# A FoX and RWKV-7 layer on one core: two operands turned by TensorE instead of VectorE and DMA

## The chip, the cores and the metric

The kernel runs on one core of one Trainium2 chip, in one launch. The metric is the time on the device in microseconds (us). The engines have short names in the profile: PE is TensorE (matmuls and transposes, PEld its weight loads), DVE is VectorE, ACT is ScalarE, POOL is GpSimd, and SP is SyncE, which issues nearly all transfers (DMAs).

## The reference

One layer on 256 frames of width 4096: a projection, two kinds of token mixing, a gate, an output projection and a normalised residual.

```python
proj = jnp.einsum('bsd,dc->bsc', x, w_in)
...
logits = jnp.einsum('bhqd,bhkd->bhqk', qb, kf) + cb[..., :, None] - c[..., None, :]
logits = jnp.where(key_pos[None, :] <= q_pos[:, None], logits, -jnp.inf)
p = jax.nn.softmax(logits, axis=-1)
return jnp.einsum('bhqk,bhkd->bhqd', p, vf)
...
sa = jnp.einsum('bhvk,bhk->bhv', state, a_t)
state = (state * w_t[:, :, None, :] + sa[..., None] * b_t[:, :, None, :]
         + v_t[..., None] * k_t[:, :, None, :])
return state, jnp.einsum('bhvk,bhk->bhv', state, r_t)
...
h = jnp.concatenate([fox_out, rwkv_out], axis=-1) * jax.nn.silu(z.astype(f32))
out = jnp.einsum('bsc,cd->bsd', h.astype(x.dtype), w_out)
x = _layernorm(ALPHA * x.astype(f32) + out.astype(f32), ln_gain, ln_bias, LN_EPS).astype(x.dtype)
```

The first three quoted parts are the projection, the forgetting attention ("fox", 16 heads of 128) and the RWKV-7 recurrence (32 heads of 64). All of it is float32.

## The kernel before, in words

**The projection sets the frame.** `w_in` is worked off in eight iterations n = 0 to 7 of four blocks b = 0 to 3, each 512 columns wide. A block is 16 chunks of weights, 512 KB each. A chunk arrives by a DMA on SP (`load`, four buffers), ACT casts it to a high half (`split`, L140, four buffers), and DVE subtracts that from the original for the low half (L141). TensorE then runs 12 matmuls of 128x512 per chunk (`mm`, L146 to L148: high by high, low by high, high by low). In the trace the halves are called `w_7h` and `w_7l` for chunk 7, whatever the block.

**The mixing runs beside it.** Every other pair of three matmuls `block` calls `slot()`, which advances each generator in `sides` by one step; a generator that yields n times (`wait(n)`, with the table `W`) so puts its next instructions n slots later in the program. Each iteration brings two RWKV groups (block 0 gives r and k, block 1 v) and two attention heads: head 2n from block 2, head 2n+1 from block 3. The generators are `prepare` (operands of the recurrence), `rwkv` (the recurrence), `unload` (turning a block's result), and `fox` (one attention head). A scheduler then orders the instructions of every engine by when it expects them to be ready; each engine works its queue in order, and a waiting instruction holds all behind it.

**In `rwkv`** the factors BK (128 x 2 x 4 chunks x 128) feed the products `gp` (L517), are scaled by POOL (L519, three of the four chunks), and are wanted transposed as `BKt` in the chunk-by-chunk recurrence (`up`, L653). They are turned in two stages: DVE transposes their 32x32 squares in place (L547), and DMAs carry the squares to their places, four to a DRAM buffer (`turn`) and one back. These DMAs are issued in `turns()`, a generator that advances with each step of the solve loop. That loop (L577 to L585) inverts the unit triangles: 31 steps of a product `prod` (L579) and a sum `xc` (L582) on DVE. It falls into block 3. The triangle's other helpers, `vt` and `bon` (L565), follow in `turns()`.

**In `fox`** the probabilities `lg` (three blocks of 128x128: DVE L722, L723, L726, ACT's exponential L724) are wanted transposed as `pT` for the product with the values, `fop` (L744, L745). For heads 0 to 13 this is done with DVE squares (L728), `turn` and a DMA back; for heads 14 and 15 with three TensorE transposes into PSUM (`fpt`, L739) and one ACT copy (L740). ACT copies `fop` out as `fo` (L747), and the gate follows.

After the iterations the output projection runs (`wo`, 128 chunks), with the residual and the norm.

Of the kernel before, what the change touches and what calls it, by code (L numbers as in the profile page):

```python
# [10 lines left out]
F32 = mybir.dt.float32  # L11
# [6 lines left out]
P = 128  # L18
# [66 lines left out]
def layer(ctx: ExitStack, tc: tile.TileContext, xt, xtok, w_lora, w_main, muv, w_o, up, par, mulora, fbias, lng, lnb, cst, out):  # L85
    nc = tc.nc
# [8 lines left out]
    def pst(name):  # L95
        return ps.tile([P, 512], F32, tag="ps", name=name)
# [34 lines left out]
    ident = cs[:, C_ID : C_ID + P]  # L131
    ones = cs[:, C_ONES : C_ONES + P]

    def column(name, i):
        return prm[:, PAR.index(name), i : i + 1]
# [21 lines left out]
    for n, (k0, k1) in enumerate(pieces):  # L157
        for k in range(k0, k1):
            t = xpool.tile([P, 2, S], F32R, tag=f"x{k}", name=f"x{k}")
# [31 lines left out]
    def wait(n):  # L191
        for _ in range(n):
            yield
# [67 lines left out]
    rp = mid.enter_context(tc.tile_pool(name="rp", bufs=1))  # L261
# [18 lines left out]
    def issue(out, src):  # L280
        tc.keep_in_program_order(nc.sync.dma_start(out=out, in_=src))

    def turn(src, name, each=2):
        _, m, cols = src.shape
        d = dram.tile([cols // B, B, m, 4, B], F32, tag=f"dt{m}_{cols}", name=name, bufs=2)
        s = src.rearrange("p m (q t) -> p m q t", t=B)
        for a in range(4):
            issue(d[:, :, :, a, :].rearrange("q i m t -> i m q t"), s[B * a : B * (a + 1)])
            if a % each == each - 1:
                yield  # L290
        return d
# [103 lines left out]
    def flat(t):  # L395
        return t.rearrange("p a b -> p (a b)")
# [108 lines left out]
    def rwkv(n):  # L505
# [3 lines left out]
        q = pairs[n]  # L509
        lc, BK, lt, bon = q["lc"], q["BK"], q["lt"], q["bon"]  # L510
# [9 lines left out]
        p, t = bks[n], vs_[n]  # L520
# [22 lines left out]
        SV = [rp.tile([P, 2, NCH, C], F32, tag=f"SV{j}", name=f"SV{j}_{n}") for j in range(2)]  # L543
        UV = [rp.tile([P, 2, NCH, C], F32, tag=f"UV{j}", name=f"UV{j}_{n}") for j in range(2)]
        yield from wait(W["tp"])
        for u in range(2):
            tc.keep_in_program_order(nc.vector.transpose(flat(BK[:, u]), flat(BK[:, u])))  # L547
        yield from wait(W["d1"])
        BKt = rp.tile([P, 2, NCH, P], F32, tag="shl", name=f"BKt{n}")

        def turns():
            d = yield from turn(BK.rearrange("p u c t -> p (u c) t"), f"BKt{n}", 1)
            yield from wait(2)
            issue(BKt.rearrange("p u c t -> p (u c t)"), d.rearrange("q i g a t -> (q i) (g a t)"))
            yield
            vst = UV[0].rearrange("p u c v -> p (u c v)").rearrange("p (m q) -> p m q", m=2)
            for a in range(2):
                tc.keep_in_program_order(nc.vector.transpose(vst[:, a, :], vs_[n][:, a, :]))
            yield from wait(3)
            d = yield from turn(vst, f"vt{n}", 1)  # L560
            yield from wait(2)
            vv[n] = rp.tile([P, 2, S], F32, tag="s2", name=f"vv{n}")
            issue(vv[n], turned_back(d))
            yield from wait(4)
            nc.vector.tensor_tensor(flat(bon), flat(bon), flat(vv[n]), ALU.mult)  # L565
            for u in range(2):
                nc.scalar.activation(bon[:, u], bon[:, u], AF.Identity, bias=column("gn_bias", i0 + u))
            bonned.add(n)
# [43 lines left out]
        for u in range(2):  # L612
            for c in range(NCH):
                for j in range(2):
                    a, b = slice(C * j, C * j + B), slice(C * j + B, C * j + C)
# [91 lines left out]
    def fox(i, q, k, vt):  # L707
        nb = rp.tile([P, 3, P], F32, tag="nb", name=f"nb{i}")
        row = ncd[i : i + 1, :]
        nc.sync.dma_start(out=flat(nb[:, 0:1, :]), in_=row[:, :P].to_broadcast([P, P]))  # L710
        nc.sync.dma_start(out=flat(nb[:, 1:3, :]), in_=row.to_broadcast([P, S]))
        for m in (0, 2):
            nc.gpsimd.affine_select(out=nb[:, m, :], in_=nb[:, m, :], compare_op=ALU.is_ge, fill=NEG, base=0, pattern=[[-1, P]], channel_multiplier=1)
        yield from wait(W["fs"])
        sp = pst(f"fsp{i}")
        nc.tensor.matmul(sp[:, :P], q[:, :P], k[:, :P], start=True, stop=True)
        nc.tensor.matmul(sp[:, P : 3 * P], q[:, P:], k, start=True, stop=True)
        lg = rp.tile([P, 3, P], F32, tag="lg", name=f"lg{i}")
        spv = sp[:, : 3 * P].rearrange("p (a t) -> p a t", t=P)
        st = rp.tile([P, 6], F32, tag="fst", name=f"fst{i}", bufs=2)  # L720
        for m, blk in enumerate((slice(0, 1), slice(1, 3))):
            nc.vector.scalar_tensor_tensor(lg[:, blk, :], spv[:, blk, :], ct[:, m * NF + i : m * NF + i + 1], nb[:, blk, :], ALU.add, ALU.add)  # L722
            nc.vector.tensor_reduce(st[:, m : m + 1], lg[:, blk, :], AX.XY, ALU.max, negate=True)  # L723
            nc.scalar.activation(lg[:, blk, :], lg[:, blk, :], AF.Exp, bias=st[:, m : m + 1], accum_out=st[:, 2 + m : 3 + m])  # L724
            nc.vector.reciprocal(st[:, 4 + m : 5 + m], st[:, 2 + m : 3 + m])
            nc.vector.tensor_scalar(lg[:, blk, :], lg[:, blk, :], st[:, 4 + m : 5 + m], None, ALU.mult)  # L726
        if i < G - 2:
            nc.vector.transpose(flat(lg), flat(lg))  # L728
        yield from wait(W["fp"])
        if i < G - 2:  # L730
            ld = yield from turn(lg, f"fpt{i}")
            yield
        pT = rp.tile([P, 3 * P], F32, tag="nb", name=f"pT{i}")
        if i < G - 2:
            issue(pT, ld.rearrange("q i m a t -> (q i) (m a t)"))
        else:
            pt = pst(f"fpt{i}")
            for m in range(3):
                nc.tensor.transpose(pt[:, m * P : (m + 1) * P], lg[:, m, :], ident)  # L739
            nc.scalar.copy(pT, pt[:, : 3 * P])  # L740
        yield from wait(W["fo"])
        op = pst(f"fop{i}")
        f = slice(i % 2 * P, i % 2 * P + P)
        nc.tensor.matmul(op[:, :S], vt[:, 0, f], pT[:, :S], start=True, stop=False)  # L744
        nc.tensor.matmul(op[:, P:S], vt[:, 1, f], pT[:, S:], start=False, stop=True)  # L745
        o = t256("fq", f"fo{i}")
        nc.scalar.copy(o, op[:, :S])  # L747
        while f"f{i}" not in szs or 2 * i >= FAR and not closed:
            yield
        yield from gate(o, f"f{i}", 2 * i)  # L750
        foxed.add(i)
# [17 lines left out]
    def turned_back(d):  # L769
        return d.rearrange("(u b) i m a t -> u (b i) (m a t)", b=4).rearrange("u p s -> p u s")  # L770
# [148 lines left out]
    for b, q in outs:  # L919
        if q == 0:  # L920
            pool, tag = (ps, "ps") if b == 1 or b and b % 2 == 0 else (pp, "pp")
# [91 lines left out]
    z0, _, last = moments(0)  # L1013
# [79 lines left out]
```

## Time and profile before

| | us |
|---|---|
| three runs, median (lowest to highest) | 1992.68 (1992.07 to 1992.7) |
| the profiled execution, its span | 1990.4 |
| what the median has over that span | 2.3 |
| one iteration, between first `gp` matmuls (n = 2 to n = 3) | 198.0 |
| PE busy | 1948.0 |
| DVE busy | 1384.1 |
| ACT busy | 962.3 |

The profiled execution has no time of its own beside its span; the runs' median is 2.3 us above it. Busy times are shares of the span: a TensorE matmul counts as busy while it runs, at full clock or not. The views that carry the argument stand in the prediction: the page, the list of waits, the timeline, the windows, and groups of instructions of one line (with count, shortest, median and longest duration in ns).

### The profile page before, as it was taken

To read this page: it belongs to the slowest core of one execution; us is meant where nothing else is said; L and a number is where in the kernel's file an instruction comes from. 1 tells how busy PE (TensorE), PEld (TensorE's weight loads), DVE (VectorE), ACT (ScalarE), POOL (GpSimd) and SP (SyncE) were. 2 spreads that over 40 slices of the span, in tenths; PEclk is the share of its full clock that TensorE was granted. 3 is DMA by queue.
4 is the path that set the end of the run, shared out by engine and by line. 5 is a ranking of instruction groups with operands and counts; after the bars stand their busy time and mean duration, and the time that the engine had idled before them with its cause. 6 is when DMAs were issued, how large, how long until landed. Compare 5 with 4: busy or idle time off the path is not lost.

```text
span 1990.4 us, 28153 instructions
## 1 busy us (share of the span) xinstructions
PE 1948.0 (98%) x10063; PEld 1583.7 (80%) x10063; DVE 1384.1 (70%) x2242; ACT 962.3 (48%) x1455; POOL 79.6 (4%) x111
## 2 busy tenths in 40 slices
PE   9998999999999999999999999999999999999998
PEld 8887787788777887778777877787778878888886
DVE  6577658865886588668866886688668856755555
ACT  6552555355535554455355544554455445443333
POOL 0010001000100010001000100010001000000000
PEclk9999999999999999999999999999999999999999
DMA  9577676867786769677867786778676877866664
GB/s 335 150 230 218 196 196 214 237 205 201 224 240 202 211 212 247 201 204 213 251 200 200 219 248 198 201 221 246 197 203 210 262 281 234 259 200 200 196 190 169
DMA packets 328241, 434.03 MB, mean 218 GB/s; under 512 B 198370, under 2 KB 228852, under 8 KB 328100
## 3 DMA queue, kind: packets, MB, share of 16 engines
q1 hardware_dynamic: 327668, 431.81, 72.3%
q8 instruction: 79, 1.29, 0.3%
q14 instruction: 62, 0.51, 0.1%
q10 hardware_dynamic: 432, 0.43, 0.1%
HBM read 395.56 MB, written 36.59 MB: 217 GB/s over the span
## 4 chain that ended last, share of the span: by engine, by line
PE 85%; DVE 11%; issue 2%; ACT 1%; DMA 1%; ACTq 0%; DVEq 0%; SPq 0%
PE acc L146 20%; PE acc L148 20%; PE acc L147 19%; PE oacc L860 6%; PE oacc L861 6%; PE oacc L862 6%; DVE prod L579 3%; DVE xc L582 3%; PE yp L678 1%; PE gp L517 1%; DMA w<-in_w_main_dram 1%; PE up L653 1%; PE rh L626 1%; DVE w_7l L141 1%; DVE w_15l L141 0%
## 5 line engine op out<-in xcount | busy, mean ns | idle before, releaser
L582 DVE TENSOR_REDUCE xc<-prod 128x8 f32<-128x16 f32 (+30 forms) x248 | 72.8, 294 | 7.0
L579 DVE TENSOR_TENSOR prod<-Nb,xc 128x8 f32<-128x8 f32 (+30 forms) x248 | 72.1, 291 | 7.0
L141 DVE TENSOR_TENSOR w_0l<-w,w_0h 128x1024 fp32r<-128x1024 f32 x31 | 37.8, 1220 | 53.0 <-ACT w_0h L140 46.9
L140 ACT CAST w_0h<-w 128x1024 fp32r<-128x1024 f32 x31 | 32.6, 1053 | 74.6 <-DMA w<-in_w_main_dram 63.6
L146 PE MATMUL acc<-w_7h,x 128*128 128x512 f32 x124 | 55.8, 450 | 10.6 <-ACT w_7h L140 10.6
L141 DVE TENSOR_TENSOR w_6l<-w,w_6h 128x1024 fp32r<-128x1024 f32 x31 | 37.9, 1222 | 35.9 <-ACT w_6h L140 19.3
L148 PE MATMUL acc<-w_7l,x 128*128 128x512 f32 x124 | 54.4, 439 | 7.9 <-DVE w_7l L141 7.9
L148 PE MATMUL acc<-w_1l,x 128*128 128x512 f32 x124 | 49.1, 397 | 7.7 <-DVE w_1l L141 7.7
L141 DVE TENSOR_TENSOR w_7l<-w,w_7h 128x1024 fp32r<-128x1024 f32 x31 | 37.9, 1224 | 26.8 <-ACT w_7h L140 16.4
L898 ACT COPY bk<-acc 128x512 f32<-128x512 f32 x48 | 28.0, 586 | 57.8 <-PE acc L148 57.6
L140 ACT CAST w_5h<-w 128x1024 fp32r<-128x1024 f32 x31 | 32.6, 1051 | 46.3 <-PE acc L147 24.5
L147 PE MATMUL acc<-w_7h,x 128*128 128x512 f32 x124 | 53.8, 434 | 0.0
L141 DVE TENSOR_TENSOR w_10l<-w,w_10h 128x1024 fp32r<-128x1024 f32 x31 | 37.9, 1223 | 22.0 <-PE acc L148 18.2
L141 DVE TENSOR_TENSOR w_5l<-w,w_5h 128x1024 fp32r<-128x1024 f32 x31 | 37.9, 1222 | 22.0 <-PE acc L148 13.5
L141 DVE TENSOR_TENSOR w_12l<-w,w_12h 128x1024 fp32r<-128x1024 f32 x31 | 37.5, 1211 | 21.8 <-PE acc L148 9.0
L141 DVE TENSOR_TENSOR w_8l<-w,w_8h 128x1024 fp32r<-128x1024 f32 x31 | 37.7, 1217 | 19.6 <-ACT UV L656 13.5
L141 DVE TENSOR_TENSOR w_11l<-w,w_11h 128x1024 fp32r<-128x1024 f32 x31 | 37.9, 1221 | 19.4 <-PE acc L148 12.0
L146 PE MATMUL acc<-w_15h,x 128*128 128x512 f32 x124 | 49.8, 401 | 1.5 <-ACT w_15h L140 1.5
L146 PE MATMUL acc<-w_8h,x 128*128 128x512 f32 x124 | 50.3, 406 | 0.8 <-ACT w_8h L140 0.8
L146 PE MATMUL acc<-w_9h,x 128*128 128x512 f32 x124 | 49.0, 395 | 1.6 <-ACT w_9h L140 1.6
L146 PE MATMUL acc<-w_5h,x 128*128 128x512 f32 x124 | 50.6, 408 | 0.0
L148 PE MATMUL acc<-w_5l,x 128*128 128x512 f32 x124 | 48.3, 398 | 2.1 <-DVE w_5l L141 2.1
(811 smaller groups left out, 6479.7 us busy)
## 6 DMA issues: line engine op xcount, KB each, us to landing
w<-in_w_main_dram SPq DMA_DIRECT2D x496, 512.0 KB
wo<-in_w_o_dram SPq DMA_DIRECT2D x128, 512.0 KB
bt<-bk SPq DMA_DIRECT2D x88, 128.0 KB
Nb<-nd SPq DMA_DIRECT2D x16, 512.0 KB
wr<-in_w_main_dram SPq DMA_DIRECT2D x15, 512.0 KB
hd<-hl SPq DMA_DIRECT2D x29, 256.0 KB
h<-hd SPq DMA_DIRECT2D x29, 256.0 KB
raw<-bt SPq DMA_DIRECT2D x16, 256.0 KB
```

The costliest lines, as they stand in the source:

```text
L140: nc.scalar.copy(hi[:, :n], src[:, :n])
L141: nc.vector.tensor_tensor(lo[:, :n], src[:, :n], hi[:, :n].bitcast(F32), ALU.subtract)
L146: nc.tensor.matmul(acc[:, :n], xs[k][:, 0, tt], hi[:, o : o + n], start=(k == 0), stop=False)
L147: nc.tensor.matmul(acc[:, :n], xs[k][:, 1, tt], hi[:, o : o + n], start=False, stop=False)
L148: nc.tensor.matmul(acc[:, :n], xs[k][:, 0, tt], lo[:, o : o + n], start=False, stop=(k == KT - 1))
L517: nc.tensor.matmul(gp[u][j][:, c * P : (c + 1) * P], BK[h, u, c, :], lt[j][h, u, c, :], start=True, stop=True)
L579: first = nc.vector.tensor_tensor(prod[:, :, :, s + 1 :], nb[:, :, s : s + 1, s + 1 :].to_broadcast([P, 2, NJ, w]), xc[:, :, :, s + 1 :], ...
L582: nc.vector.tensor_reduce(xc[:, :, :, s : s + 1], prod[:, :, :, s:], AX.X, ALU.add)
L860: nc.tensor.matmul(acc, ht[k][:, 0, tt], hi, start=(k == 0), stop=False)
L861: nc.tensor.matmul(acc, ht[k][:, 1, tt], hi, start=False, stop=False)
L862: nc.tensor.matmul(acc, ht[k][:, 0, tt], lo, start=False, stop=(k == KT - 1))
L898: nc.scalar.copy(bk[:, m, :], acc[m])
```

## The change

BK is turned by TensorE: for each of the two groups three 128x128 transposes into one PSUM tile and one ACT copy of 128x384. The fourth chunk isn't turned, as nothing reads it. The step stands where the DVE squares stood, behind `wait(W["tp"])` and ahead of `wait(W["d1"])`. In `turns()` the four DMAs to DRAM, the one back and seven yields go. In `fox` all 16 heads take the path that heads 14 and 15 had; its squares, DMAs and three yields go for the others. It is 90 transposes and 30 ACT copies more, and 30 DVE transposes and 110 DMAs fewer.

```diff
@@ rwkv @@
         yield from wait(W["tp"])
+        BKt = rp.tile([P, 2, NCH - 1, P], F32, tag="shl", name=f"BKt{n}")
         for u in range(2):
-            tc.keep_in_program_order(nc.vector.transpose(flat(BK[:, u]), flat(BK[:, u])))
+            bt = pst(f"bkt{n}_{u}")
+            for c in range(NCH - 1):
+                nc.tensor.transpose(bt[:, c * P : (c + 1) * P], BK[:, u, c, :], ident)
+            nc.scalar.copy(flat(BKt[:, u]), bt[:, : (NCH - 1) * P])
         yield from wait(W["d1"])
-        BKt = rp.tile([P, 2, NCH, P], F32, tag="shl", name=f"BKt{n}")
 
         def turns():
-            d = yield from turn(BK.rearrange("p u c t -> p (u c) t"), f"BKt{n}", 1)
-            yield from wait(2)
-            issue(BKt.rearrange("p u c t -> p (u c t)"), d.rearrange("q i g a t -> (q i) (g a t)"))
-            yield
@@ fox @@
-        if i < G - 2:
-            nc.vector.transpose(flat(lg), flat(lg))
         yield from wait(W["fp"])
-        if i < G - 2:
-            ld = yield from turn(lg, f"fpt{i}")
-            yield
         pT = rp.tile([P, 3 * P], F32, tag="nb", name=f"pT{i}")
-        if i < G - 2:
-            issue(pT, ld.rearrange("q i m a t -> (q i) (m a t)"))
-        else:
-            pt = pst(f"fpt{i}")
-            for m in range(3):
-                nc.tensor.transpose(pt[:, m * P : (m + 1) * P], lg[:, m, :], ident)
-            nc.scalar.copy(pT, pt[:, : 3 * P])
+        pt = pst(f"fpt{i}")
+        for m in range(3):
+            nc.tensor.transpose(pt[:, m * P : (m + 1) * P], lg[:, m, :], ident)
+        nc.scalar.copy(pT, pt[:, : 3 * P])
         yield from wait(W["fo"])
```

The scheduler moves other instructions with it. In the rows below `w3_1_7h` is the high half of chunk 7 of block 1 in iteration 3, `acc3_1_0` that block's sum, and `x` the layer's input; the numbers behind a name tell tiles apart.

**TensorE, iteration 3, block 1.** Before, the product `fop5` of head 5 stands inside chunk 6:

```order
L146 MATMUL acc3_1_0_6297<-w3_1_6h_6401,x13_440 128x512
L147 MATMUL acc3_1_0_6297<-w3_1_6h_6401,x13_440 128x512
L744 MATMUL fop5_6411<-pT5_6375,vt2_4927 128x256
L745 MATMUL fop5_6411<-pT5_6375,vt2_4927 128x128
L148 MATMUL acc3_1_0_6297<-w3_1_6l_6402,x13_440 128x512
L146 MATMUL acc3_1_1_6298<-w3_1_6h_6401,x13_440 128x512
L147 MATMUL acc3_1_1_6298<-w3_1_6h_6401,x13_440 128x512
L148 MATMUL acc3_1_1_6298<-w3_1_6l_6402,x13_440 128x512
L146 MATMUL acc3_1_0_6297<-w3_1_7h_6429,x14_475 128x512
```

Now it stands between chunks 2 and 3:

```order
L146 MATMUL acc3_1_1_6293<-w3_1_2h_6296,x5_288 128x512
L147 MATMUL acc3_1_1_6293<-w3_1_2h_6296,x5_288 128x512
L148 MATMUL acc3_1_1_6293<-w3_1_2l_6297,x5_288 128x512
L735 MATMUL fop5_6371<-pT5_6336,vt2_4923 128x256
L736 MATMUL fop5_6371<-pT5_6336,vt2_4923 128x128
L146 MATMUL acc3_1_0_6292<-w3_1_3h_6326,x6_323 128x512
L147 MATMUL acc3_1_0_6292<-w3_1_3h_6326,x6_323 128x512
```

and its new transposes `fpt5` (a row that stands for three) in the middle of chunk 1:

```order
L147 MATMUL acc3_1_1_6293<-w3_1_1h_6254,x2_247 128x512
L148 MATMUL acc3_1_1_6293<-w3_1_1l_6255,x2_247 128x512
L730 MATMUL fpt5_6337<-cs_72,lg5_6240 128x128 x3
L146 MATMUL acc3_1_0_6292<-w3_1_1h_6254,x3_250 128x512
L147 MATMUL acc3_1_0_6292<-w3_1_1h_6254,x3_250 128x512
```

So `fop5` has moved ahead by 44 matmuls of the projection, with `fpt5` 18 matmuls ahead of it.

**ACT, the same place.** Before, the copy `fo5` of that product stands between the casts of chunks 6 and 7:

```order
L418 CAST uph7_6591<-upt7_6273 96x256
L140 CAST w3_1_5h_6381<-w3_1_5_6329 128x1024
L140 CAST w3_1_6h_6401<-w3_1_6_6354 128x1024
L747 COPY fo5_6414<-fop5_6411 128x256
L379 CAST hl10_6418<-h10_6416 128x256
L140 CAST w3_1_7h_6429<-w3_1_7_6379 128x1024
L140 CAST w3_1_8h_6466<-w3_1_8_6399 128x1024
```

Now, with the new copy `pT5` some rows ahead:

```order
L140 CAST w3_1_4h_6352<-w3_1_4_6294 128x1024
L731 COPY pT5_6336<-fpt5_6337 128x384
L480 COPY lc3_6448<-eL6_6309 128x4
L418 CAST uph7_6585<-upt7_6268 96x256
L140 CAST w3_1_5h_6385<-w3_1_5_6324 128x1024
L140 CAST w3_1_6h_6405<-w3_1_6_6350 128x1024
L738 COPY fo5_6374<-fop5_6371 128x256
L379 CAST hl10_6378<-h10_6376 128x256
L140 CAST w3_1_7h_6424<-w3_1_7_6383 128x1024
```

`fo5` stands between the same two casts as before, while the product that it copies comes earlier on TensorE.

**DVE, iteration 2, block 3, the end of the solve loop.** `prod2` and `xc2` are its steps (the last figure grows with them, 31 is the last), `w2_3_5l` the low half of chunk 5. Before:

```order
L579 TENSOR_TENSOR prod2_5191<-Nb2_5057,xc2_5192 128x8x29
L582 TENSOR_REDUCE xc2_5192<-prod2_5191 128x8
L579 TENSOR_TENSOR prod2_5191<-Nb2_5057,xc2_5192 128x8x30
L582 TENSOR_REDUCE xc2_5192<-prod2_5191 128x8
L579 TENSOR_TENSOR prod2_5191<-Nb2_5057,xc2_5192 128x8x31
L582 TENSOR_REDUCE xc2_5192<-prod2_5191 128x8
L141 TENSOR_TENSOR w2_3_5l_5405<-w2_3_5_5348,w2_3_5h_5404 128x1024
L141 TENSOR_TENSOR w2_3_6l_5433<-w2_3_6_5373,w2_3_6h_5432 128x1024
L565 TENSOR_TENSOR bon2_4666<-bon2_4666,vv2_5398 128x512
L141 TENSOR_TENSOR w2_3_7l_5460<-w2_3_7_5402,w2_3_7h_5459 128x1024
L141 TENSOR_TENSOR w2_3_8l_5483<-w2_3_8_5430,w2_3_8h_5482 128x1024
```

Now:

```order
L141 TENSOR_TENSOR w2_3_6l_5434<-w2_3_6_5376,w2_3_6h_5433 128x1024
L578 TENSOR_TENSOR prod2_5195<-Nb2_5053,xc2_5196 128x8x27
L581 TENSOR_REDUCE xc2_5196<-prod2_5195 128x8
L578 TENSOR_TENSOR prod2_5195<-Nb2_5053,xc2_5196 128x8x28
L581 TENSOR_REDUCE xc2_5196<-prod2_5195 128x8
L578 TENSOR_TENSOR prod2_5195<-Nb2_5053,xc2_5196 128x8x29
L581 TENSOR_REDUCE xc2_5196<-prod2_5195 128x8
L578 TENSOR_TENSOR prod2_5195<-Nb2_5053,xc2_5196 128x8x30
L581 TENSOR_REDUCE xc2_5196<-prod2_5195 128x8
L578 TENSOR_TENSOR prod2_5195<-Nb2_5053,xc2_5196 128x8x31
L581 TENSOR_REDUCE xc2_5196<-prod2_5195 128x8
L141 TENSOR_TENSOR w2_3_7l_5458<-w2_3_7_5403,w2_3_7h_5457 128x1024
```

The low halves of chunks 5 and 6 stood behind the loop's last step, and `bon2` with them; now chunk 6's stands ahead of the last five steps, chunk 5's further ahead, and chunk 7's right behind the loop.

## The prediction

> **What bounds the kernel now.** I read the page of the profile first, for the engine that sets the time. These are its rows of busy time, of granted clock, and of the chain that ended last.
>
> ```profile
> PE 1948.0 (98%) x10063; PEld 1583.7 (80%) x10063; DVE 1384.1 (70%) x2242; ACT 962.3 (48%) x1455; POOL 79.6 (4%) x111
> PEclk9999999999999999999999999999999999999999
> PE 85%; DVE 11%; issue 2%; ACT 1%; DMA 1%; ACTq 0%; DVEq 0%; SPq 0%
> ```
>
> TensorE (PE) is the bound: whatever the change adds to PE is paid, and all it can win are the places where PE stands still or runs slowly. The busy share hides part of the latter, as a matmul at half clock counts as busy. So the second view is the list of PE's waits (what was waited for: us in total, times, longest).
>
> ```profile
> PE acc L146 <- ACT w_7h L140: 10.6, 7, 2.3
> PE acc L148 <- DVE w_7l L141: 7.9, 8, 4.2
> PE acc L148 <- DVE w_1l L141: 7.7, 8, 1.5
> PE acc L148 <- DVE w_5l L141: 2.1, 7, 0.8
> PE acc L146 <- ACT w_9h L140: 1.6, 1, 1.6
> PE acc L146 <- ACT w_15h L140: 1.5, 1, 1.5
> ...
> PE acc L148 <- DVE w_15l L141: 0.5, 1, 0.5
> ```
>
> Nearly all of it is for a weight chunk's high half (cast by ACT) or low half (subtracted by DVE), at the same chunks in each of the eight iterations. The third view is the timeline at the costliest place, chunks 6 to 8 of block 1, iteration 2 (columns: start, length, engine, line, operation, idle before it and its releaser).
>
> ```profile
> 494.08 0.39 PE L146 MATMUL acc<-w_6h,x 128*128 128x512 f32 x1
> ...
> 495.89 0.59 PE L744 MATMUL fop<-pT,vt 128*128 128x256 f32 x2
> 496.32 0.38 PE L745 MATMUL fop<-pT,vt 128*128 128x128 f32 x2
> 496.46 0.48 PE L148 MATMUL acc<-w_6l,x 128*128 128x512 f32 x1
> 496.74 0.37 ACT L747 COPY fo<-fop 128x256 f32<-128x256 f32 x1 [8.50 <-PE fop L745]
> 496.78 0.39 PE L146 MATMUL acc<-w_6h,x 128*128 128x512 f32 x1
> ...
> 497.92 1.04 ACT L140 CAST w_7h<-w 128x1024 fp32r<-128x1024 f32 x1
> ...
> 499.01 0.50 PE L146 MATMUL acc<-w_7h,x 128*128 128x512 f32 x1 [1.38 <-ACT w_7h L140]
> ...
> 500.27 0.54 PE L148 MATMUL acc<-w_7l,x 128*128 128x512 f32 x1 [0.53 <-DVE w_7l L141]
> 500.61 0.63 PE L146 MATMUL acc<-w_7h,x 128*128 128x512 f32 x1
> ...
> 504.25 0.39 PE L146 MATMUL acc<-w_8h,x 128*128 128x512 f32 x1
> ```
>
> ACT stands 8.50 us at the copy `fo`, since PE reaches `fop` only behind the eighth matmul of chunk 6. The cast of `w_7h` is queued behind that copy, so it comes late. PE waits 1.38 + 0.53 us, and then runs slowly. Its usual pace is eight matmuls from 494.08 to 495.89, 0.227 us each; the nine from 500.61 to 504.25 take 0.404 each. From chunk 6 to chunk 8 go 504.25 - 494.08 = 10.17 us, where two chunks of 12 matmuls (5.44 us) and `fop` (0.57 us to 496.46, and 0.09 more until 496.78) ask for 6.10. So **stall A costs 4.07 us** each time, of which 1.91 are idle and some 2.2 are the slow clock. The granted clock stands beside it in the table of windows (us; PE, PEld, DVE, ACT and POOL busy; PEclk, DMA share, GB/s):
>
> ```profile
> 501.60:504.25 2.65, 2.65 (x8) 2.04 (x7) 2.65 (x7) 2.06 (x4) 0.11 (x1) 0.55 0.73 199
> ```
>
> The next place is block 3, chunk 1, where the solve loop (L579, L582) keeps DVE busy: the timeline, and the window around it.
>
> ```profile
> 576.55 1.22 DVE L141 TENSOR_TENSOR w_1l<-w,w_1h 128x1024 fp32r<-128x1024 f32 x1
> ...
> 577.83 0.50 PE L148 MATMUL acc<-w_1l,x 128*128 128x512 f32 x1 [0.96 <-DVE w_1l L141]
> ...
> 557.00:579.00 22.00, 21.04 (x93) 17.13 (x92) 20.30 (x55) 9.17 (x10) 0.00 (x0) 1.00 0.80 232
> ```
>
> DVE is busy 20.30 of 22 us; `w_1l` is late because DVE has too much ahead of it. The granted clock is 1.00 in that window, so 0.96 us of idleness did not lower it, and **stall B** costs its idle time.
>
> **The change part by part.** The transposes that go to PE: 8 × 6 of BK and 14 × 3 of `lg`, 90 in all. Before has such ones in the last iteration, so their price can be read in place.
>
> ```profile
> 1568.90 0.60 PE L815 MATMUL tr<-cs,bk 128*128 128x128 f32 x4
> 1569.26 0.48 PE L146 MATMUL acc<-w_1h,x 128*128 128x512 f32 x1
> 1569.58 0.40 PE L147 MATMUL acc<-w_1h,x 128*128 128x512 f32 x1
> ...
> L739 PE MATMUL fpt<-cs,lg x6: 272/273/328, 1586.9 to 1644.7; 128*128 128x128 f32 x6
> L740 ACT COPY pT<-fpt x2: 481/482/482, 1587.4 to 1645.1; 128x384 f32<-128x384 f32 x2
> ```
>
> Four transposes and one matmul take from 1568.90 to 1569.58, 0.68 us; less the matmul's 0.23 that is 0.45, or **0.113 us each**. The recorded 273 ns are latency, which overlaps. 90 × 0.113 = **+10.2 us** on the path. Bounds: 0.113 below (in a full queue they cannot come cheaper, and they cannot cost less than nothing), 0.273 above, 24.6 us. I take the lower, since a group of three or four inside a stream of matmuls is just what is added.
>
> The Trainium skill speaks against the change here: "TensorE: Matmul & The Clock Gate", section "Part 4: PE-mode transpose", gives about 275 ns for a transpose in a kernel's context, and says that it does not count as busy for the clock. By that figure the estimate would be 90 × 0.275 = 24.8 us, and the forecast 14.6 us later. The trace disagrees on both: after the four transposes matmuls follow 0.23 us apart.
>
> PSUM copies on ACT: 16 + 14 of 128x384 at 0.482 us (L740 above) are 14.5 us over the kernel, on an engine that is 48% busy. I cost them at nothing, since they stand between casts which run chunks ahead of PE; without that cover they would cost up to those 14.5 us.
>
> Removed from DVE and from SP:
>
> ```profile
> L547 DVE STREAM_TRANSPOSE BK<-BK x16: 660/680/698, 153.4 to 1540.2; 128x512 f32<-128x512 f32 x16
> L728 DVE STREAM_TRANSPOSE lg<-lg x14: 548/575/579, 201.2 to 1471.4; 128x384 f32<-128x384 f32 x14
> ...
> BKt<-BK SPq DMA_DIRECT2D x32, 128.0 KB
> ...
> fpt<-lg SPq DMA_DIRECT2D x56, 48.0 KB
> ```
>
> DVE gets rid of 16 × 0.680 + 14 × 0.575 = 18.9 us, and SP of these 88 DMAs and the 22 that read them back. Neither bounds the kernel by its sum, so this counts only through PE's waits. POOL's queue and its multiply of BK stay where they were. Seven yields go from the loop's second generator and three from each attention head, so what follows comes earlier in every queue:
>
> - `fop` of the odd heads moves from the middle of chunk 6 to the end of chunk 2, 44 matmuls or some 10 us earlier. `fo` keeps its place in ACT's queue ahead of `w_7h`, but no longer waits 8.50 us there, so I expect `w_7h` to be cast as soon as a buffer is free, some three chunks (8 us) ahead. Stall A goes: 7 × 4.07 = 28.5, and 0.9 more for the longest (2.3 for 1.38): **−29.4 us**. What is late next there is `lg`, below.
> - In block 3 DVE's queue now has the subtractions of chunks 1 to 6 inside the solve loop and many steps earlier, and `w_7l` right behind the loop. Stall B's 7.7 us go, and of `w_5l`'s 2.1 all but the longest, 0.8, which I leave standing: 7.7 + 1.3 = **−9.0 us**. Bounds: nothing, if the loop's end merely moves the wait to `w_7l`, and −9.0. I take −9.0, as DVE loses 1.36 us of squares in that stretch and SP the turn that its waits stood for.
> - The first iteration's `w_9h` now stands ahead of the steps that held it (−1.6); in the last, `qt` goes behind chunk 15, so the copy `Q` no longer holds `w_15h` and `w_15l` (−2.0): **−3.6 us**.
> - The longest wait for `w_7l` (4.23 us, in the first iteration's block 3, the row at 191.61 below) stays, since the loop still stands ahead of it, and the product `bon` now does too. I estimate +1.3: one operation of DVE about as long as `w_7l`'s own subtraction (1.22 in the row of `w_1l`). Bounds: −1.4, the two squares that DVE is rid of, and +1.3.
> - New waits: PE's queue now holds `fpt` and `fop` behind `lg`, with all matmuls queued behind. In block 1 before, the last step of `lg` and the matmul at which `fpt` will stand are these; in block 3, the same step of `lg`; the wait for `w_7l` goes with them:
>
> ```profile
> 191.61 0.79 PE L148 MATMUL acc<-w_7l,x 128*128 128x512 f32 x1 [4.23 <-DVE w_7l L141]
> ...
> 678.72 0.35 DVE L726 TENSOR_SCALAR lg<-lg,fst 128x256 f32<-128x256 f32 x1
> 679.76 0.39 PE L146 MATMUL acc<-w_1h,x 128*128 128x512 f32 x1
> ...
> 803.27 0.34 DVE L726 TENSOR_SCALAR lg<-lg,fst 128x256 f32<-128x256 f32 x1
> ```
>
> In block 1 `lg` is ready at 679.07, 0.69 us before PE. In block 3 it is ready at 803.61; PE would be two matmuls into chunk 11 at about 804.4, less the 1.2 to 1.5 us that it gains in the block: a tie. I allow 0.5 us in each of seven iterations, **+3.5 us**; bounds nothing and 1.0 each.
>
> Sum: 10.2 − 29.4 − 9.0 − 3.6 + 1.3 + 3.5 = −27.0. The profiled span of 1990.4 us becomes 1963.4; the median of the runs, 1992.7, lies 2.3 above that span, so the time is **1965.7 us**.
>
> **The rivals.**
>
> *The loop stays the bound in block 3.* For it: DVE busy 20.30 of 22 us; a wait of PE there that is taken away lets PE run into the next late subtraction, `w_7l` at the loop's end. Against it: `w_7l` is needed 16 us after `w_1l`, and DVE's queue is shorter. Then the 9.0 us are not won: 1974.7.
>
> *Transposes cost their recorded length*, 0.273 us. For it: that row alone. Against it are the starts at 1568.90 and 1569.26. Then 14.4 more: 1980.1.
>
> *Stall A has another cause.* Were `w_7h` late for its load, it would stay: 1965.7 + 29.4 = 1995.1, no change by 0.2% of this kernel (4 us), which is about what a measurement can tell. Against it: the cast's row at 497.92 has no idle time of its own; ACT's wait stands at `fo`.
>
> *A wait for `lg` takes A's place, slower than before.* PE stands at `fpt` in order, so a late `lg` stops everything. It decides at the idle time at which the clock falls: 1.38 + 0.53 us did it at 499, 0.96 at 577.83 didn't. If in block 3 `lg` is 1.9 us or more behind PE, each costs A's 4.07, 7 × 4.07 = 28.5, and if in block 1 it is 1 us late, 7 more; the 3.5 already allowed come off: 1965.7 + 32 = 1997.7. For it: the tie in block 3, and DVE busy nearly throughout. Against: the margin of 0.69 in block 1, and that `lg` needs 2 us more than a tie to do it.
>
> The Trainium skill ("TensorE: Matmul & The Clock Gate", "Part 1: The HAM clock gate") lets the clock fall only after an idle window of about 3.4 us; by that rule this rival would need longer waits and would be rarer. The trace disagrees: the granted clock was 0.55 after 1.91 us of idleness in two parts.
>
> **How the numbers follow.** Forecast (1959 to 1971) 0.55; the loop stays the bound (1974.7) 0.18; transposes at full length (1980.1) 0.07; more won than I count, the first iteration's `w_7l` too (1956) 0.05; A stays (1995.1) 0.07; a wait for `lg` (1997.7) 0.08. Faster by over 0.2%: 0.55 + 0.18 + 0.07 + 0.05 = 0.85; the same 0.07; slower 0.08. The low end is the sum without new waits and with `w_7l` shortened: 1965.7 − 3.5 − 2.7 = 1959.5, and 2.2 below that for `w_7l`'s slow clock, 1957. The high end takes in the loop as bound and transposes at full length, 1980, and 2 for new waits at 0.3 above what I allow: 1982. Outside lie 0.05 + 0.07 + 0.08 = 0.2.
>
> **What would show it.** Right: among PE's waits no row for `w_7h`, and for `w_1l` under 1 us; at `w_7h`'s cast ACT some 8 us ahead of PE; from chunk 6 to chunk 8 of block 1 some 5.5 us; a granted clock of 1.00 in those windows; groups of three transposes costing 0.34 us by the starts around them; DVE's busy time some 19 us down, ACT's 14 up. Wrong: new rows with `fpt` or `w_7l` in the waits of PE at over 1 us an iteration, granted clock of half around them, or matmuls that follow the transposes late.

## The result and the profile after

The changed kernel takes 1956.6 us (median of four runs, 1954.7 to 1957.6) where the kernel before takes 1992.4 us beside it (four runs, 1985.2 to 1992.7). The ratio is 0.9824, with a 95% interval of 0.9806 to 0.9842: faster by 1.8%, some 35 us, where 27 were forecast. The profiled execution took 1955.92 us with a span of 1954.0.

The page of the changed kernel answers to the rows shown of before:

```profile
PE 1935.8 (99%) x10153; PEld 1585.4 (81%) x10153; DVE 1366.9 (70%) x2212; ACT 978.4 (50%) x1485; POOL 79.9 (4%) x111
...
PE 95%; DVE 3%; DMA 1%; ACT 0%; issue 0%; DVEq 0%; SPq 0%; ACTq 0%
```

TensorE runs 90 instructions more and is busy 12 us less, since matmuls at half clock had counted as busy. In the chain that ended last, DVE's share fell from 11% to 3%. The list of PE's waits in the changed kernel:

```profile
PE acc L148 <- DVE w_7l L141: 5.8, 1, 5.8
...
PE fpt L730 <- DVE lg L725: 0.2, 1, 0.2
```

No row for `w_7h`, `w_1l`, `w_5l`, `w_9h` or `w_15h` is left. Of the new waits, 0.2 us came. The one long wait is the first iteration's `w_7l`. Iterations 1 to 6, between first `gp` matmuls, took 197.9 to 198.4 us and take 193.4 to 193.9.

Here is block 1 of iteration 2, where stall A stood, in ACT's timeline, and PE's first matmuls of chunks 6 and 8:

```profile
480.61 0.36 ACT L738 COPY fo<-fop 128x256 f32<-128x256 f32 x1
481.46 0.41 ACT L379 CAST hl<-h 128x256 fp32r<-128x256 f32 x1 [0.49 <-DVE h L376]
482.45 1.06 ACT L140 CAST w_7h<-w 128x1024 fp32r<-128x1024 f32 x1 [0.58 <-PE acc L147]
...
487.92 0.39 PE L146 MATMUL acc<-w_6h,x 128*128 128x512 f32 x1
493.36 0.39 PE L146 MATMUL acc<-w_8h,x 128*128 128x512 f32 x1
```

`fo` has no idle time ahead of it, where it had 8.50 us; `w_7h` waits for a buffer only (0.58 us, freed by a matmul) and is cast 8.2 us ahead of chunk 7's start at 490.64. The two chunks take 5.44 us, 24 matmuls at 0.227, where they and `fop` took 10.17. They take 5.44 in each of the seven iterations; before, what those two chunks took above 6.10 was 4.98 us in iteration 1 and 4.03 to 4.08 in the others, 29.4 us together.

The transposes that the change put on TensorE, and what their rows record:

```profile
152.80 0.82 PE L550 MATMUL bkt<-cs,BK 128*128 128x128 f32 x6
153.37 0.48 PE L146 MATMUL acc<-w_11h,x 128*128 128x512 f32 x1
153.69 0.40 PE L147 MATMUL acc<-w_11h,x 128*128 128x512 f32 x1
...
L550 PE MATMUL bkt<-cs,BK x48: 270/272/273, 152.8 to 1506.2; 128*128 128x128 f32 x48
```

Six of them and one matmul take 0.89 us; less 0.227, that is 0.66, or 0.111 us each. The record of 272 ns is again the length of one, not its cost.

The one stall that is left, the first iteration's chunk 7 (the timeline, then the window behind it, whose third figure from the end is PEclk):

```profile
190.84 0.68 DVE L564 TENSOR_TENSOR bon<-bon,vv 128x512 f32<-128x512 f32 x1
191.43 1.22 DVE L141 TENSOR_TENSOR w_7l<-w,w_7h 128x1024 fp32r<-128x1024 f32 x1
...
192.71 0.80 PE L148 MATMUL acc<-w_7l,x 128*128 128x512 f32 x1 [5.75 <-DVE w_7l L141]
...
192.00:198.00 6.00, 5.29 (x13) 4.18 (x14) 3.68 (x5) 5.05 (x8) 0.00 (x0) 0.50 0.62 178
```

`w_7l` stands behind the loop's last step and `bon`, and the clock is at 0.50 afterwards.

### The profile page after: what moved, and what is told of

It is laid out like the page before. It is cut to its first block, busy times and chain, and to the rows that moved or that the text cites. A ratio compares the mean times of both kernels' runs of the same rounds, so it can differ in the third digit from the quotient of the medians.

```text
span 1954.0 us, 28165 instructions
## 1 busy us (share of the span) xinstructions
PE 1935.8 (99%) x10153; PEld 1585.4 (81%) x10153; DVE 1366.9 (70%) x2212; ACT 978.4 (50%) x1485; POOL 79.9 (4%) x111
## 4 chain that ended last, share of the span: by engine, by line
PE 95%; DVE 3%; DMA 1%; ACT 0%; issue 0%; DVEq 0%; SPq 0%; ACTq 0%
PE acc L146 24%; PE acc L148 23%; PE acc L147 23%; PE oacc L851 6%; PE oacc L853 6%; PE oacc L852 6%; PE yp L677 1%; PE gp L517 1%; PE up L652 1%; PE rh L625 1%; PE sp L661 0%; DVE xc L581 0%; DVE prod L578 0%; PE fsp L716 0%; PE fop L735 0%
## 5 line engine op out<-in xcount | busy, mean ns | idle before, releaser
L140 ACT CAST w_7h<-w 128x1024 fp32r<-128x1024 f32 x31 | 32.6, 1052 | 48.3 <-PE acc L147 28.8
L148 PE MATMUL acc<-w_7l,x 128*128 128x512 f32 x124 | 48.6, 400 | 5.8 <-DVE w_7l L141 5.8
L140 ACT CAST w_13h<-w 128x1024 fp32r<-128x1024 f32 x31 | 32.6, 1052 | 37.1 <-DMA w<-in_w_main_dram 17.9
L146 PE MATMUL acc<-w_7h,x 128*128 128x512 f32 x124 | 51.0, 411 | 0.0
L141 DVE TENSOR_TENSOR w_14l<-w,w_14h 128x1024 fp32r<-128x1024 f32 x31 | 38.2, 1231 | 17.3 <-issue 10.9
L146 PE MATMUL acc<-w_3h,x 128*128 128x512 f32 x124 | 50.3, 405 | 0.0
L140 ACT CAST w_8h<-w 128x1024 fp32r<-128x1024 f32 x31 | 32.5, 1050 | 34.8 <-DMA w<-in_w_main_dram 24.5
L140 ACT CAST w_10h<-w 128x1024 fp32r<-128x1024 f32 x31 | 32.5, 1047 | 34.8 <-PE acc L147 32.6
L146 PE MATMUL acc<-w_6h,x 128*128 128x512 f32 x124 | 49.9, 402 | 0.0
```

The lines of the kernel that those rows point to most:

```text
L140: nc.scalar.copy(hi[:, :n], src[:, :n])
L141: nc.vector.tensor_tensor(lo[:, :n], src[:, :n], hi[:, :n].bitcast(F32), ALU.subtract)
L146: nc.tensor.matmul(acc[:, :n], xs[k][:, 0, tt], hi[:, o : o + n], start=(k == 0), stop=False)
L148: nc.tensor.matmul(acc[:, :n], xs[k][:, 0, tt], lo[:, o : o + n], start=False, stop=(k == KT - 1))
```

## The experiments

All ratios are against the kernel before, run beside each on the same chip.

**The two halves.** e1 keeps the change's `fox` and takes `rwkv` of before; e2 the other way round.

> The change's attention part alone (42 transposes more), BK turned as before. My theory: stall A (the wait for w_7h) goes and the waits for w_1l and w_5l stay, so 1992.4 - 29.4 + 42 x 0.113 = 1967.7 us; the list of waits has no w_7h and some 7.7 us for w_1l. Rival, the gain comes from the work and the transfers that DVE and SP are rid of, wherever they lie: this part has 8 of 18.9 us of DVE's and 70 of 110 DMAs, so about half of the 36 us, some 1974 us, with both kinds of wait shortened.

> The change's BK part alone (48 transposes more), attention's probabilities turned as before. My theory: w_7h's 10.6 us and the slow clock behind them stay, the waits for w_1l and w_5l go: 1992.4 - 9.0 + 48 x 0.113 = 1988.8 us. Rival (relief of DVE and SP, wherever it lies): about half of the 36 us, some 1974 us.

e1: 1966.5 us, ratio 0.9875 (0.9859 to 0.9890). e2: 1981.2 us, ratio 0.9946 (0.9933 to 0.9958). The lists of PE's waits, first of the attention part alone, then of the BK part alone:

```profile
PE acc L148 <- DVE w_1l L141: 8.7, 7, 2.2
PE acc L148 <- DVE w_7l L141: 4.2, 1, 4.2
PE acc L148 <- DVE w_5l L141: 2.1, 7, 0.9
```

```profile
PE acc L146 <- ACT w_7h L140: 10.6, 7, 2.3
PE acc L148 <- DVE w_7l L141: 9.4, 8, 5.7
```

Each part takes away its own waits and leaves the other's, and by these lists the even split of the rival falls. By the time alone e1 is 1.2 us from my theory, but e2 lies between: 7.6 us under my 1988.8 and 7.2 above the rival's 1974. My figure for e2 had left out `w_9h` and `w_15h`, whose waits go there too (3.6 us), and had stall B too small, as shown below; in iteration 4 of e2 the clock also did not fall behind stall A (chunk 7 took 3.66 us in place of 4.87 to 5.25; the last section shows why). The parts win 24.9 and 10.8 us by the ratios, 35.7 together, where the whole wins 35.1: they add up. With their transposes' 4.7 and 5.3 us put back, the attention part is worth 29.6 us and the BK part 16.1; the 1.6 us of `w_9h` are in both.

**What in BK's turn made stall B: DVE's squares, or the DMAs?** e3 is the changed kernel with the squares put back on DVE (their result unread):

```diff
         yield from wait(W["tp"])
+        for u in range(2):
+            tc.keep_in_program_order(nc.vector.transpose(SV[u].rearrange("p u c v -> p (u c v)"), flat(BK[:, u])))
         BKt = rp.tile([P, 2, NCH - 1, P], F32, tag="shl", name=f"BKt{n}")
```

> The changed kernel, and DVE transposes BK's squares as before all the same (16 x 0.68 us, into a tile that is overwritten later, so nothing reads them); no DMA comes back. The rows of the solve loop stand in DVE's queue as in the changed kernel. Theory 1, DVE's work in block 3 made the waits for w_1l and w_5l: they return, 5 to 9 us, 1962 to 1966 us. Theory 2, the place of the low halves among the loop's steps made them: within 2 us of the changed kernel, 1956 to 1959 us, no wait for w_1l.

e4 puts the DMAs and yields back instead (their result unread too):

```diff
         def turns():
+            d = yield from turn(BK.rearrange("p u c t -> p (u c) t"), f"BKd{n}", 1)
+            yield from wait(2)
+            for h in range(2):
+                issue(SV[h].rearrange("p u c v -> p (u c v)"), d.rearrange("q i (h g) a t -> h (q i) (g a t)", h=2)[h])
+            yield
             vst = UV[0].rearrange("p u c v -> p (u c v)").rearrange("p (m q) -> p m q", m=2)
```

> The changed kernel, and BK is carried to DRAM and back by DMAs with their seven yields all the same (into tiles that are overwritten later, so nothing reads them); DVE's squares stay away. With these DMAs the low halves of chunks 1 to 6 stand at the places in DVE's queue that they had before. Theory 1 (DVE's work): no wait for w_1l, 1956 to 1959 us. Theory 2 (the places in the queue): w_1l's 7 us and w_5l's 1 return, some 1964 to 1966 us.

e3: 1955.2 us, 0.9819 (0.9805 to 0.9832), the changed kernel's time. e4: 1972.3 us, 0.9906 (0.9892 to 0.9920), 16 us slower than the changed kernel and 6 above my range. The waits of PE in e4:

```profile
PE acc L148 <- DVE w_1l L141: 7.0, 7, 1.2
PE acc L148 <- DVE w_7l L141: 4.6, 1, 4.6
PE acc L148 <- DVE w_5l L141: 2.5, 7, 0.5
PE acc L146 <- ACT w_15h L140: 1.5, 1, 1.5
```

DVE's 11 us of squares are worth nothing. The DMAs with their yields bring stall B back, and more time than I expected: chunks 1 and 5 of block 3 take 1.92 us longer than in the changed kernel in each of iterations 1 to 6, and the last iteration's waits for `w_15h` and `w_15l`, 2.0 us, are back as well. The idle time understates the stall. In the kernel before, chunk 1 of block 3 in iteration 2 goes from 576.25 to 580.23:

```profile
576.25 0.39 PE L146 MATMUL acc<-w_1h,x 128*128 128x512 f32 x1
...
580.23 0.39 PE L146 MATMUL acc<-w_2h,x 128*128 128x512 f32 x1
...
588.52 0.39 PE L146 MATMUL acc<-w_5h,x 128*128 128x512 f32 x1
...
591.75 0.39 PE L146 MATMUL acc<-w_6h,x 128*128 128x512 f32 x1
```

That is 3.98 us, 1.26 over the 2.72 of twelve matmuls, where the recorded wait was 0.96; chunk 5 takes 3.23 us, 0.51 over, with a recorded wait of 0.21. Together 1.77 us an iteration, or 12.4 us in seven, against 8.2 by the waits. A wait is counted from the end of the last row, and rows overlap: the third matmul of chunk 1 was due at 576.70, 0.227 us behind the second, whose row lasts 0.39; it starts 1.13 us late, not 0.96, and the next one follows it by 0.33.

What the DMAs change is the order of rows, on ACT and on DVE. First ACT's timeline, of the kernel before and of the changed one, where block 2 of iteration 2 ends:

```profile
572.41 0.59 ACT L898 COPY bk<-acc 128x512 f32<-128x512 f32 x1 [5.95 <-PE acc L148]
573.73 0.59 ACT L898 COPY bk<-acc 128x512 f32<-128x512 f32 x1 [0.73 <-PE acc L148]
574.21 1.05 ACT L140 CAST w_1h<-w 128x1024 fp32r<-128x1024 f32 x1
```

```profile
557.85 1.05 ACT L140 CAST w_1h<-w 128x1024 fp32r<-128x1024 f32 x1 [1.66 <-PE acc L147]
...
562.20 0.59 ACT L889 COPY bk<-acc 128x512 f32<-128x512 f32 x1 [0.58 <-PE acc L148]
```

Before, `w_1h` was queued on ACT behind the two copies `bk` of the finished block, which wait for its last matmuls: ACT stood 5.95 us, and cast `w_1h` at 574.21, 2.0 us ahead of PE. In the changed kernel `w_1h` stands ahead of those copies, 8.2 us ahead of PE.

The late cast alone does not make PE wait. `w_1h` was done at 575.26, and a subtraction of 1.22 us begun then would have ended at 576.48, ahead of the 576.70 at which PE wanted `w_1l`. The rest is DVE's queue, before and now (with the cast of `w_5h` on ACT):

```profile
575.34 0.70 DVE L789 STREAM_TRANSPOSE bk<-bk 128x512 f32<-128x512 f32 x1
...
581.44 1.06 ACT L140 CAST w_5h<-w 128x1024 fp32r<-128x1024 f32 x1 [3.34 <-DVE xc L582]
...
588.20 0.42 DVE L582 TENSOR_REDUCE xc<-prod 128x8 f32<-128x256 f32 x1
588.54 1.22 DVE L141 TENSOR_TENSOR w_5l<-w,w_5h 128x1024 fp32r<-128x1024 f32 x1
```

```profile
561.72 1.22 DVE L141 TENSOR_TENSOR w_1l<-w,w_1h 128x1024 fp32r<-128x1024 f32 x1
...
563.77 0.70 DVE L780 STREAM_TRANSPOSE bk<-bk 128x512 f32<-128x512 f32 x1
...
572.95 1.22 DVE L141 TENSOR_TENSOR w_5l<-w,w_5h 128x1024 fp32r<-128x1024 f32 x1
```

Before, a transpose of `bk` and two rows of the loop stood between the end of that cast and `w_1l`, which DVE took up at 576.55 without having been idle; now `w_1l` stands ahead of the transposes of `bk`. `w_5l` is a matter of DVE's queue alone: its high half was cast seven microseconds ahead, and it stood behind the loop's last step. So stall B is the order of rows in both queues, not the amount of DVE's work.

In all kernels of this study ACT's rows stand in the first order where stall B is there (before, e1, e4, e5, e9) and in the second where it is not (the changed kernel, e2, e3, e6, e7, e8, e10, e11, e12). With the yields there in both, the DMAs in SP's queue decide which order the scheduler writes (e4 against e8 below); those DMAs on SP without the yields were not run. That the order alone makes the stall, with the same DMAs, was not tried, nor was ACT's order apart from DVE's.

**Is stall A the late product, or what is queued behind its copy?** e5 is the kernel before with `fo` on DVE:

```diff
-        nc.scalar.copy(o, op[:, :S])
+        nc.vector.tensor_copy(o, op[:, :S])
```

> The kernel before, with one line changed: DVE instead of ACT copies fop out of PSUM (fo). fop stays in the middle of chunk 6, and no transposes come to TensorE. My theory, stall A is made by ACT's queue (the cast of w_7h behind the waiting copy): the row for w_7h goes, and DVE, which waits for fop now as it waited for fo before, still has w_7l some 0.5 us late, without a fall of the clock; 29 less 7 x 0.5, so 1991.4 - 26 = 1965 us. Rival, the late fop itself or the loads behind the turn's DMAs make the wait: w_7h keeps its 10.6 us, 1991 us.

1991.6 us, 1.0001 (0.9989 to 1.0012): nothing. ACT's timeline of e5 shows why:

```profile
496.67 0.40 ACT L379 CAST hl<-h 128x256 fp32r<-128x256 f32 x1 [10.71 <-DVE h L376]
496.98 1.04 ACT L140 CAST w_7h<-w 128x1024 fp32r<-128x1024 f32 x1
```

The next step behind `fop`, the cast `hl` of the gated head, also stands ahead of `w_7h`; ACT waits there instead. So the run left the suspected cause in place and told nothing against it. e9 moves both steps to DVE, `fo` as in e5 and `hl` so:

```diff
-        nc.scalar.copy(hl[:, 0, :], h)
+        if key[0] == "f":
+            nc.vector.tensor_copy(hl[:, 0, :], h)
+        else:
+            nc.scalar.copy(hl[:, 0, :], h)
```

> The kernel before with both of ACT's steps behind fop moved to DVE: the copy fo and the cast of the gated head (hl, attention heads only). In the run with fo alone on DVE, ACT stood 10.71 us at hl instead, ahead of the same cast of w_7h. Now nothing on ACT ahead of w_7h waits for fop, which stays in the middle of chunk 6. My theory (ACT's queue): the row for w_7h goes; DVE has four small steps, some 1.5 us, between fop and w_7l, so w_7l is 0.5 to 1 us late without a fall of the clock; 7 x 3.3 us won, 1965 to 1970 us. Rival (the late fop itself, or late loads): w_7h keeps some 10 us, 1991 us.

1983.0 us, 0.9957 (0.9943 to 0.9971). The timeline of e9 at the same place, and two windows (PEclk is again the third figure from the end):

```profile
493.38 1.05 ACT L140 CAST w_7h<-w 128x1024 fp32r<-128x1024 f32 x1 [6.64 <-DMA w<-in_w_main_dram]
...
496.54 0.43 DVE L750 COPY fo<-fop 128x256 f32<-128x256 f32 x1 [6.62 <-PE fop L748]
...
498.13 1.22 DVE L141 TENSOR_TENSOR w_7l<-w,w_7h 128x1024 fp32r<-128x1024 f32 x1
...
499.40 0.49 PE L148 MATMUL acc<-w_7l,x 128*128 128x512 f32 x1 [1.50 <-DVE w_7l L141]
...
499.00:501.60 2.60, 2.20 (x10) 1.82 (x11) 2.60 (x6) 0.29 (x1) 0.00 (x0) 1.00 0.47 82
501.60:505.00 3.40, 3.40 (x17) 2.81 (x16) 3.37 (x8) 3.29 (x5) 0.11 (x1) 1.00 0.78 262
```

`w_7h` is in time, so ACT's queue was the cause of that wait; but now DVE stands at `fo` with `w_7l` behind it, and PE waits 1.50 us for that (2.43 in iteration 1). I had put it at 0.5 to 1, and the time at 1965 to 1970. The clock did not fall there. The wait was handed on to the next queue: over the seven iterations stall A shrinks from 29.4 us to 13.8 by the length of chunks 6 and 7. Of the 15.6 us so won 8.4 are left, since e9 loses time elsewhere: 0.3 us in block 0 of most iterations, and a fall of the clock at 203 and another at 1599 us that the kernel before doesn't have.

e11 goes the other way: the changed kernel with `fop` of the odd heads put back into chunk 6; the scheduler places `fo` behind `w_7h` there.

```diff
-        yield from wait(W["fo"])
+        yield from wait(W["fo"] + 7 * (i % 2))
```

> The changed kernel with fop of the odd heads put off by seven slots, to the middle of chunk 6 where it stood before; its copy fo now stands behind w_7h in ACT's queue, where it stood ahead of it before. My theory: a late fop costs nothing when no cast that is needed soon is behind it; w_8h, which is, is cast some 1.5 us before PE needs it: 1955 to 1959 us. Rival, the place of fop on TensorE is what the change wins by: 4 us an iteration come back, some 1985 us.

1954.7 us, 0.9818 (0.9802 to 0.9834), the changed kernel's time. ACT's timeline of e11:

```profile
480.53 1.06 ACT L140 CAST w_7h<-w 128x1024 fp32r<-128x1024 f32 x1 [1.66 <-PE acc L147]
...
488.21 0.37 ACT L738 COPY fo<-fop 128x256 f32<-128x256 f32 x1 [6.62 <-PE fop L736]
```

ACT stands 6.62 us at `fo`, where it was 8.50 in the kernel before, and it costs nothing, since `w_7h` is in front: chunks 6 and 7 with `fop` inside take 6.13 us in every iteration, against 10.17. So stall A needs both, a late `fop` and the cast of `w_7h` behind its copy. The change took away the first and left the two rows in their order; e11 takes away the second.

**The price of a transpose.** e6 issues each of the new transposes (and those of heads 14 and 15) twice, with this line ahead of both:

```diff
+                for _ in range(2):
                     nc.tensor.transpose(bt[:, c * P : (c + 1) * P], BK[:, u, c, :], ident)
```

> The changed kernel with each of the new transposes issued twice into the same place (96 more, with those of heads 14 and 15). At 0.113 us each, 10.8 us more, 1967.4 us; at their recorded 0.273 us, 26 more, 1983 us; were they hidden in gaps, 1956.6.

1965.4 us, 0.9870 (0.9855 to 0.9885): 8.8 us for 96, 0.09 each; between the extreme runs of the two kernels lie 6.9 to 12.2 us, 0.07 to 0.13 each. That agrees with 0.111 from the timeline, and rules out 0.27.

**The last stall.** e7 starts the first iteration's loop earlier, and e8 puts the seven yields back into `turns()`, without DMAs; the first edit is e7's, the second e8's:

```diff
-        yield from wait(W["d1"])
+        yield from wait(W["d1"] if n else 4)
...
         def turns():
+            yield from wait(7)
```

> The changed kernel with the solve loop of the first iteration started four slots earlier (wait of 4 in place of W[d1] = 8 for n = 0 alone). The wait for w_7l there, 5.75 us and then half a clock (some 8 us lost), is the one long wait that is left. If DVE's work from the loop's start bounds it, the loop can start at about 158.5, when its operand has landed, in place of 163.0, and has two low halves more inside: it ends some 2 us earlier, and bon stands ahead; the wait falls to 3.3 us, 1953 to 1954 us. If the loop's operand is the bound, nothing changes: 1956.6.

> The changed kernel with the seven yields of the old turn put back ahead of the value's turn in turns(), without its DMAs. In the first iteration w_7l then stands two steps ahead of the loop's end and bon behind it; in later ones the low halves stand as in the changed kernel. If it was the yields that set the old places of the low halves, w_1l's waits come back, 1964 us; if it was the DMAs on SP, they do not, and w_7l comes some 2.4 us earlier in the first iteration: 1952 to 1955 us.

e7: 1956.9 us, 0.9826 (0.9810 to 0.9841), no change. Its timeline has the reason, DVE at the loop's first step:

```profile
162.56 0.17 DVE L578 TENSOR_TENSOR prod<-Nb,xc 128x8 f32<-128x8 f32 x1 [3.29 <-DMA Nb<-nd]
```

The operand lands at 162.5, not at 158.5; the loop cannot start earlier. e8: 1963.5 us, 0.9857 (0.9841 to 0.9873), 7 us slower than the changed kernel. The second case holds for the order, not for the time: `w_1l` stays away, and the first iteration's `w_7l` waits 2.7 us in place of 5.8, but in six later iterations a wait of some 0.5 us for `w_7l` comes, which I had not foreseen; chunks 6 and 7 take 1.2 us longer there. ACT's and DVE's rows in e8:

```profile
581.63 0.91 ACT L567 ACTIVATE bon<-bon,prm 128x256 f32<-128x256 f32 x2 [8.19 <-DVE bon L565]
583.51 1.22 DVE L141 TENSOR_TENSOR w_7l<-w,w_7h 128x1024 fp32r<-128x1024 f32 x1 [1.59 <-ACT w_7h L140]
```

With the yields, `bon` comes at the loop's end, ACT stands 8.19 us at the step that reads it, and `w_7h` is behind that: stall A's pattern once more. The kernel before has the same yields and not this wait, so e8 doesn't tell what part of the change's gain comes from the yields.

**Are the transposes needed at all?** e10 keeps the change's `fox`, and turns BK as before, by squares and DMAs, but issues these from POOL without yields (the part in `turns()`, against the kernel before):

```diff
-            d = yield from turn(BK.rearrange("p u c t -> p (u c) t"), f"BKt{n}", 1)
-            yield from wait(2)
-            issue(BKt.rearrange("p u c t -> p (u c t)"), d.rearrange("q i g a t -> (q i) (g a t)"))
-            yield
+            src = BK.rearrange("p u c t -> p (u c) t")
+            d = dram.tile([4, B, 8, 4, B], F32, tag="dBK", name=f"BKd{n}", bufs=2)
+            s4 = src.rearrange("p m (q t) -> p m q t", t=B)
+            for a in range(4):
+                nc.gpsimd.dma_start(out=d[:, :, :, a, :].rearrange("q i m t -> i m q t"), in_=s4[B * a : B * (a + 1)])
+            nc.gpsimd.dma_start(out=BKt.rearrange("p u c t -> p (u c t)"), in_=d.rearrange("q i g a t -> (q i) (g a t)"))
```

> The change's attention part, and BK turned as before by DVE's squares and five DMAs, but these issued from POOL and not from SP, without their yields. The 48 transposes of BK are not on TensorE, and the low halves stand in DVE's queue as in the changed kernel. If the place of the low halves is all that the BK part wins by, its waits stay away and 48 x 0.111 = 5.3 us are saved: 1951.3 us, faster than the changed kernel. If the transfers themselves (their small packets beside the loads) cost, some of the 9 us comes back: 1955 to 1962 us.

1952.6 us, 0.9804 (0.9789 to 0.9820). The waits for `w_1l` and `w_5l` stay away, and most iterations take 192.8 to 193.0 us in place of 193.4 to 193.6: some 0.6 us, about six transposes' worth. e12 does the same with the probabilities, so none of the 90 transposes is left, and puts `fop` off, which places `fo` behind `w_7h` (only this last edit is shown):

```diff
-        yield from wait(W["fo"])
+        yield from wait(W["fo"] + 8)
```

> The kernel before, without any of the change's transposes: BK and the probabilities are turned by DVE's squares and DMAs, all issued from POOL in place of SP, and fop is put off by eight slots, so that it stands at the end of chunk 6 with its copy fo behind w_7h in ACT's queue. My theory (the two places in the queues are all that the change wins by): 1952.6 - 42 x 0.111 = 1948, plus 0.3 to 1 us in each iteration where w_8h or the transfer of pT comes late: 1949 to 1955 us, no wait for w_7h and none for w_1l but for small ones. Rival (the transposes on TensorE, with no transfer between lg and fop, are needed): PE waits at fop or for w_8h by more than 1.9 us an iteration, the clock falls, and some 4 us an iteration come back: 1975 us and more.

1950.8 us, 0.9798 (0.9780 to 0.9816), inside my range and the fastest median of the study, though its interval overlaps the changed kernel's. So the transposes on TensorE are not needed for the gain. Its list of PE's waits:

```profile
PE acc L148 <- DVE w_7l L141: 9.7, 4, 6.9
...
PE fpt L743 <- DVE lg L728: 1.1, 1, 1.1
```

## Why the prediction was right, and where not

The direction and the two stalls were right, the size was not: the change won 35 us where 27 were forecast. 1956.6 us lies below the band of 1959 to 1971, which had a chance of 0.55, and at the low edge of the whole range, 1957 (0.9824 of the 1992.7 that the forecast started from is 1957.6). One case named this time, "more won than I count, the first iteration's `w_7l` too (1956)", with a chance of 0.05, but it didn't come: that wait grew. The time came out there for other reasons, so its closeness to 1956 is luck. Term by term:

- *Price of the transposes*: right. 0.113 us was forecast, 0.111 is read in place, and e6 gives 0.09 (0.07 to 0.13). By the figure of about 275 ns in the Trainium skill, "TensorE: Matmul & The Clock Gate", section "Part 4: PE-mode transpose", the estimate would have been 24.8 us. The rows do record 272 ns, but that is not what a transpose costs in a stream of matmuls. The granted clock of the changed kernel fell at two places only, behind the first iteration's `w_7l` and at the kernel's end, and so at none of the groups of transposes between.
- *Stall A*: right in place, mechanism and size. 29.4 us were forecast; the trace shows 29.4 by the length of chunks 6 and 7, and e1 29.6 with `w_9h` in it. The text gave the earlier `fop` as what removes it. That is how this change does it; e11 and e12 show that a late `fop` does as well, if `fo` stands behind `w_7h`.
- *Stall B*: right that it goes, half right in why, too small in size. The step that failed is that "DVE loses 1.36 us of squares in that stretch" as a reason for the gain: e3 gives DVE that work back and loses nothing. The other reasons hold, the low halves' earlier places in DVE's queue and SP's turn (e4). "`w_1l` is late because DVE has too much ahead of it" is true of the last microsecond, a transpose of `bk` and two rows of the loop; the cast of `w_1h`, late behind ACT's copies `bk`, was overlooked. And "stall B costs its idle time" took 0.96 and 0.21 where the chunks lost 1.26 and 0.51: 12.4 us instead of the 9.0 of the sum.
- *`w_9h` and `w_15h`*: both waits went, as forecast (3.6 us by their idle time).
- *The first iteration's `w_7l`*: forecast to stay and grow by 1.3. It grew from 4.23 to 5.75 us of idleness, and its chunk by 1.3.
- *New waits for `lg`*: 3.5 us were allowed, 0.2 came; the tie in block 3 went well. This and stall B's size, 3.3 and 3.4 us, make up most of the 8 us by which the gain was more than forecast.
- *Copies on ACT*: costed at nothing. No wait for one of them is in the changed kernel's list.
- *Rivals*: the loop as a bound in block 3, transposes at full length, stall A's other cause, and a wait for `lg` in A's place: none came.

## What to carry to other kernels

An engine's queue is in order, so look not at how long an engine waits but at what stands behind the waiting instruction. ACT's wait for a late product cost PE 4 us a time with the weight cast behind it (8.50 us of waiting, the kernel before), and nothing with that cast in front (6.62 us, e11).

When a change removes work and the time falls, put the work back without its ordering before crediting the work. Here DVE's squares were free, and the transposes on TensorE were not needed. What the change won came from orders: `fop` earlier on TensorE, and, without BK's DMAs on SP, the weight steps of block 3 further ahead on ACT and DVE.

And price a stall by the time between the chunks around it, since a slow clock and the overlap of rows hide part of it from the list of waits.

## What the runs showed of the hardware that was not expected

A single wait of PE of 1.50 us left the granted clock at 1.00 (e9), while 1.38 and 0.53 us within 2.7 us took it to 0.55 (before). The idle time alone does not decide it. In e5 waits of 1.43 and 0.53 us lowered it in five of seven iterations only (chunk 7 took 3.67 us in iterations 2 and 6, and 5.10 to 5.24 in the others), and a single wait of 2.43 us left it at 1.00 (e9, iteration 1).

What the traces do show is a fixed division of time. In each of the fourteen traces all stretches of half clock start whole multiples of 3.41 us apart, and but for the last of a kernel they last 3.41 or 6.83. So cut each trace into such pieces of 3.41 us, from 80 us on and without the last 20, and take those at full clock. Behind all 31 in which PE was busy 1.66 us or less the clock was halved, behind two of the three with 1.72 to 1.73, and behind one of the 7545 with 1.82 or more (e9 at 1595.71, where 32x32 matmuls are part of the 1.88 us). In these runs, then, the clock fell when PE had been busy for less than about half of a piece. The same waits can fall into one piece or into two: in iteration 2 of the kernel before PE was busy 1.51 us from 497.19 to 500.60, and the next 3.41 us ran at 0.50; in e5 a piece ends at 498.67, between the two waits, PE was busy 1.98 us in it, and the clock stayed. This is read from the traces; no run varied it alone.

The kernels that issue small transfers from POOL were no slower than the changed one (1952.6 us in e10, 1950.8 in e12), although each issue takes POOL 0.56 to 1.01 us; POOL was busy for 4% of the span before.
